# Turning softmax weights in row halves, and a new order of an attention visit, in a two-layer trunk on one core

## The chip, the cores and the metric

The kernel runs on one core of a Trainium2 chip. The metric is the device time of one execution in microseconds (us). An execution uses five engines that run side by side and wait for each other by semaphores: TensorE (PE, matmuls; its weight loads are shown as PEld), VectorE (DVE), ScalarE (ACT), GpSimd (POOL) and SyncE (SP), which here issues the weight DMAs. Matmul results land in PSUM, eight banks of 128 partitions by 512 fp32 words; everything else lives in SBUF. Each engine works through its own queue in order.

## The reference

The reference is a trunk of two layers over 256 latent tokens with 256 context tokens, width 1024, fp32. Each layer has a token-mixing part (a gated convolution branch beside an attention branch, both after a modulated norm and one combined projection) and a gated MLP. Cut to the attention, which is where the change lies:

```
s_win = einsum("bhqd,bhiqjd->bhqij", q_r, k_win) * scale + bias      # 16-wide window over the rows
s_ctx = einsum("bhqd,bhcd->bhqc", q_r, k_ctx) * scale                # all context keys
s = concatenate([s_win, s_ctx]);  p = softmax(s)
out = p_win @ v_win + p_ctx @ v_ctx                                  # latent queries
ctx_out = softmax(q_c k_c^T * scale) @ v_c                           # context queries, layer 0 only
```

There are 8 heads of 64 channels, taken as 4 pairs. In the last layer the context tokens only give keys and values, so nothing is computed for them as queries.

## The kernel before, in words

**Projections.** Weights come as units of 128x1024 fp32 by SP (tile `raw`, four buffers). ACT rounds a unit to fp32r (`whi`, L158) and DVE subtracts that from the unit (`wlo`, L159); a product of fp32 accuracy is then three matmuls (`mm3`, L177 to L179), each of a high or low weight part with a high or low part of the activations. A projection group is eight such triples into one PSUM bank. Between triples, `slot()` lets side work take a step: the taps of the convolution (DVE, L576) and the attention's visits.

**Attention.** The class `Attention` keeps three lists: `todo` (head pairs whose q and k are there), `soft` (pairs whose softmax weights `pp` are made, or on the way) and `pv` (turned weights `pT`, waiting for their product with V). A head pair gives one latent item of two query halves of 128; every two pairs give one context item in layer 0. A call of `step` that acts is one visit. It works off what the visit before left:

- `turn` (L476): the weights `pp` are [128 queries, 512 keys] per head and query half, and the product with V wants keys on partitions. Four 128x128 transposes on PE fill one bank, and one ACT copy (L485, for context items L490) takes the bank to `pT`. A visit has four such banks: tags sc, sc, pt, main in this order.
- `values` (L494): sixteen matmuls L502 of 256 moving columns into one bank, then per item an ACT cast `oh` (L508) and a DVE subtraction `ol` (L509).
- scores: `products` (L430) multiplies q by k in three high/low products for both heads of a pair; a head has 64 channels, so the two heads sit on partitions 0 to 63 and 64 to 127 and are multiplied in row halves of the PE array. The four banks are, in order, sc, sc, pt, main. Softmax follows: for latent items DVE adds the bias and finds the extremum (L448), ACT takes the exponential (L451) and scales (L454); for context items L462, L467 and L472.

Before, a visit is issued as turn, values, scores. A visit that has no weights to turn, or no values, or no scores leaves that stage out. In layer 0 the visits with a turn are six, the last of which has no scores; in layer 1 there are four, the last again without scores. Each layer ends with a visit of values alone.

**What sets the order.** The Tile framework takes instructions in the order of the program's calls, moves them by a priority of its own within what `tc.issue_after` allows, and fills in the semaphore waits. It also hands out the PSUM buffers of each tag (`BANKS`: main 4, sc 2, pt 1, po 1) in rotation; a new user of a bank waits for the last reader of the old one. Projection groups, the rotary step of q and k (DVE L747 to L750, ACT L753, DVE L754) and the attention's third and fourth banks all share main, so which bank a group gets depends on how many were taken before it.

**Who reads the banks.** ACT's copies L485 free the banks of a turn. In the same queue ACT has the whi casts, the sigmoids of the gates (L591 with the multiplication on DVE, L799), the copies of gate projections (L613), q and k's rounding (L753) and the softmax. DVE has the taps, the wlo subtractions and the rotary step.

**After layer 0's attention.** SP loads rows for the next modulation (`sb` from `in_crow`, L243); ACT computes on them (L245), DVE multiplies (L261), and PE's next step (L224) waits for the result of ACT L217.

Of the kernel before, what the change touches and what calls it, by code (L numbers as in the profile page):

```python
# [8 lines left out]
F32 = mybir.dt.float32  # L9
# [6 lines left out]
P = 128  # L16
# [3 lines left out]
S = 256  # L20
# [12 lines left out]
LAT, CTX = slice(0, S), slice(S, 2 * S)  # L33
# [12 lines left out]
def trunk(ctx: ExitStack, tc: tile.TileContext, xt, cvec, crow, wall, wada, params, bias_t, rope_t, out):  # L46
    nc = tc.nc
    pe, act, dve, pool, sp = nc.tensor, nc.scalar, nc.vector, nc.gpsimd, nc.sync
# [11 lines left out]
    def nm(s):  # L60
        uid[0] += 1
        return f"{s}_{uid[0]}"
# [3 lines left out]
    def psum(tag="main"):  # L66
        return psp.tile([P, 512], F32, tag=tag, bufs=BANKS[tag], name=nm(tag))

    def tmp(w=512):
        return tp.tile([P, w], F32, tag="t", bufs=5, name=nm("t"))  # L70
# [4 lines left out]
    def sl(w, i):  # L75
        return w[:, i * P : (i + 1) * P]
# [29 lines left out]
    start = ExitStack()  # L106
# [5 lines left out]
    ident = cp.tile([P, P], F32, name="ident")  # L112
# [260 lines left out]
    HALF = [slice(0, HD), slice(HD, P)]  # L373

    class Attention:
# [30 lines left out]
        def step(self, now=False):  # L406
            self.n += 1
            since = self.n - self.at
            if not now and (since < (4 if self.todo else 3 if self.soft else 2) or not self.todo and self.pairs < 4):
                return  # L410
            if self.todo and not now and self.n - self.todo[0][0] < 2:
                return
            self.at = self.n
            pv, self.pv = self.pv, []
            soft, self.soft = self.soft, []
            for what, its, pps in soft:
                with tc.issue_after(self.last.ins), tc.issue_after(self.done.ins):
                    self.turn(what, its, pps)
            for work in pv:
                self.values(*work, "sc" if work[0] == CTX and not (soft or self.todo) else "po")  # L420
            if self.todo:
                _, what, its = self.todo.pop(0)
                outs = [self.products(it, [psum(t) for t in tags]) for it, tags in zip(its, (("sc", "sc"), ("pt", "main")))]
                self.soft.append((what, its, [(self.scores if what == LAT else self.ctx_scores)(it, o) for it, o in zip(its, outs)]))

        def product(self, out, q, k, c, d):
# [48 lines left out]

        def turn(self, what, its, pps):  # L476

            pts = [self.eb.tile([P, 4, S], F32, tag="pT", bufs=4, name=nm("pT")) for _ in range(2)]
            for n, tags in enumerate((("sc", "sc"), ("pt", "main"))):
                for i, pp in enumerate(pps[n]):  # L480
                    pt = psum(tags[i])
                    if what == LAT:
                        for kt in range(4):
                            pe.transpose(sl(pt, kt), sl(pp, kt), ident)
                        act.copy(pts[i][:, :, n * P : (n + 1) * P], pt.rearrange("p (k q) -> p k q", k=4))  # L485
                    else:
                        for t in range(2):
                            for kt in range(2):
                                pe.transpose(pt[:, kt * S + t * P : kt * S + (t + 1) * P], sl(pp, 2 * t + kt), ident)
                        act.copy(pts[i][:, 2 * n : 2 * n + 2, :], pt.rearrange("p (k q) -> p k q", k=2))  # L490
            js = [its[0][0]] if what == LAT else [it[0] for it in its]
            self.pv.append((what, js, pts))

        def values(self, what, js, pts, bank):  # L494
            po = psum(bank)
            kts = range(4) if what == LAT else range(2, 4)
            for n, j in enumerate(js):
                c = slice(n * S, (n + 1) * S)
                for kt in kts:
                    for i in range(2):  # L500
                        h = 2 * j + i
                        pe.matmul(  # L502
                            po[i * HD : (i + 1) * HD, c], self.V[kt][:, h * HD : (h + 1) * HD],
                            pts[i][:, 2 * n + kt - kts[0], :], start=kt == kts[0], stop=kt == kts[-1],
                        )
            for n, j in enumerate(js):
                c = slice(n * S, (n + 1) * S)
                act.copy(self.oh[j][:, what], po[:, c])  # L508
                dve.tensor_tensor(self.ol[j][:, what], po[:, c], self.oh[j][:, what].bitcast(F32), ALU.subtract)  # L509
# [11 lines left out]
    for k in range(KD):  # L521
        sp.dma_start(x[k], xt[k])
        q = tmp()
# [19 lines left out]
    for l in range(DEPTH):  # L543
# [5 lines left out]
        with ExitStack() if last else start as e1a:  # L549
# [68 lines left out]
            with ExitStack() as e1b:  # L618
# [14 lines left out]
                if l == 0:  # L633

                    pv = [psum() for _ in range(4)]
# [81 lines left out]
                else:  # L717
                    sp.dma_start(rope, rope_t)
                    pg0 = [psum("sc") for _ in range(2)]
                    for uu in range(2):  # L720
                        wg = wunit(l, U_GLU0 + uu)
                        for i in range(2):
                            for kk in range(4):
                                k = 4 * uu + kk
# [44 lines left out]
                else:  # L769
                    wvs = [wunit(l, U_V + uu) for uu in range(4)]  # L770
                    for half in range(2):
                        pv = {t: psum() for t in (2 * half, 2 * half + 1)}
# [11 lines left out]
                n = 0  # L784
# [16 lines left out]
            with ExitStack() as e1c:  # L801
# [71 lines left out]
                for n, pc in branch(U_CO, sh_, sl_):  # L873
                    t = tmp()[:, :T]
# [60 lines left out]
        with ExitStack() as e2:  # L935
# [115 lines left out]
            for streams, ns in [((0, 1), range(NB)), *(((s,), range(NB, KD)) for s in range(NS))]:  # L1051
                wu = None
                c = slice(streams[0] * S, (streams[-1] + 1) * S)
                for n in ns:
                    ps = psum()
                    for k in range(KF):
                        t = n * KF + k
# [19 lines left out]
            if last:  # L1077
                std, rs = small([P, 2], "red"), small([P, 2], "rs")
                pt = psum("pt")
# [133 lines left out]
```

## Time and profile before

| what | value |
|---|---|
| median of 3 runs | 1129.97 us (1129.38 to 1132.16) |
| profiled execution, first to last instruction | 1127.4 us |
| granted TensorE clock, mean | 0.998 |
| PE busy | 1115.5 us (99%) |
| DVE busy | 906.5 us (80%) |
| ACT busy | 565.7 us (50%) |
| turns in the run | 10, of 16 transposes each (160) |
| visits with scores | 10 |

The profiled execution's own time is its span of 1127.4 us and what lies outside the first and last instruction, which the page does not show; the median of the runs is 2.6 us above that span.

The attention's visits, as the starts of their first matmuls on PE in us (the end is the start of the next projection group):

| layer, visit | turn | values | scores | next group |
|---|---|---|---|---|
| 0, first | | | 84.24 | 85.83 |
| 0, second | 102.69 | | 104.53 | 106.32 |
| 0, third | 112.00 | 113.84 | 115.72 | 117.57 |
| 0, last turn | 192.50 | 194.34 | | 196.22 |
| 0, last values | | 199.20 | | 201.08 |
| 1, second | 812.83 | | 814.66 | 816.45 |
| 1, third | 827.82 | 829.66 | 831.53 | 833.12 |
| 1, last turn | 858.47 | 860.31 | | 862.19 |

How to read the profile's lines: a timeline row gives the start and the covered time in us, the engine, the line of the kernel, the operation, output tile <- input tiles, the shape and the count; what stands in square brackets is the idle time of that engine before the row, and what ended it. A row of one source line gives the count, the shortest, median and longest duration in ns, and the first and last start in us. A PE matmul's duration includes its fill and drain, so the distance from one start to the next is what it costs in a sequence. "128*64" behind MATMUL means 128 rows and 64 columns of the PE array in use. The chain that ended last is followed back from the last instruction through what released each step.

### The profile page before, as it was taken

Reading aid. Unit: us, or ns where it says so; the run is one execution under the profiler, and the core shown is the slowest. Engines: PE = TensorE matmul, PEld = TensorE weight load, DVE = VectorE, ACT = ScalarE, POOL = GpSimd, SP = SyncE. Lnnn points to the kernel's source line nnn. Section 1 sums busy time; section 2 is a strip of 40 time slices with the busy share of each in tenths; the row PEclk is TensorE's granted clock in tenths of the full one; section 3 lists DMA queues with packets and bytes.
Section 4 is the critical chain, followed back from the end, with each engine's and each line's share of the span. In section 5 each row is a group of like instructions: output and inputs, shape, how many; then the busy total and the mean of one; then the engine's idle time right before and its main releaser. Section 6 shows DMA issues by size and latency. Waiting matters only on the chain.

```text
span 1127.4 us, 17780 instructions
## 1 busy us (share of the span) xinstructions
PE 1115.5 (99%) x6854; PEld 965.1 (86%) x6854; DVE 906.5 (80%) x1625; ACT 565.7 (50%) x937; POOL 17.2 (2%) x24
## 2 busy tenths in 40 slices
PE   9999999999999999999999999999999999999997
PEld 7678777787789988888888888989898999999997
DVE  4689999786778788888898555789996898988773
ACT  4347657542334543444334223544677667766642
POOL 0000000000000000000000000010000000000000
PEclk9999999999999999999999999999999999999999
DMA  8832231635734354545556656555533575665781
GB/s 325 310 100 89 92 117 38 200 99 198 248 120 145 110 170 133 184 152 155 165 181 205 214 188 197 176 194 174 154 109 120 180 247 175 187 193 182 213 274 57
DMA packets 53941, 190.83 MB, mean 169 GB/s; under 512 B 6240, under 2 KB 6496, under 8 KB 53856
## 3 DMA queue, kind: packets, MB, share of 16 engines
q1 hardware_dynamic: 53568, 189.65, 52.6%
q8 instruction: 54, 0.88, 0.3%
q14 instruction: 31, 0.25, 0.1%
q10 hardware_dynamic: 288, 0.04, 0.0%
HBM read 188.62 MB, written 1.05 MB: 168 GB/s over the span
## 4 chain that ended last, share of the span: by engine, by line
PE 85%; DVE 10%; DMA 2%; ACT 2%; issue 1%; POOL 0%; SPq 0%; DVEq 0%; ACTq 0%; POOLq 0%
PE main L177 25%; PE main L179 24%; PE main L178 24%; DVE cb L576 4%; PE main L629 4%; DVE wlo L159 2%; DMA raw<-in_wall 1%; PE sc L127 1%; PE sc L177 1%; PE sc L179 1%; PE sc L178 1%; PE po L200 1%; PE po L502 1%; DMA sb<-in_crow 1%; PE sc L430 0%
## 5 line engine op out<-in xcount | busy, mean ns | idle before, releaser
L177 PE MATMUL main<-h,whi 128*128 128x256 f32 (+1 forms) x1328 | 446.8, 337 | 0.0
L179 PE MATMUL main<-h,wlo 128*128 128x256 f32 (+1 forms) x1328 | 443.4, 335 | 0.5 <-DVE wlo L159 0.5
L178 PE MATMUL main<-h,whi 128*128 128x256 f32 (+1 forms) x1328 | 442.4, 333 | 0.0
L158 ACT CAST whi<-raw 128x1024 fp32r<-128x1024 f32 (+1 forms) x244 | 252.5, 1039 | 284.7 <-PE main L178 128.6
L159 DVE TENSOR_TENSOR wlo<-raw,whi 128x1024 fp32r<-128x1024 f32 (+1 forms) x244 | 293.7, 1209 | 113.3 <-ACT whi L158 108.6
L177 PEld LDWEIGHTS main<-h,whi 128*128 128x128 f32 x1328 | 249.5, 188 | 32.0 <-issue 3.9
L179 PEld LDWEIGHTS main<-h,wlo 128*128 128x128 f32 x1328 | 249.5, 188 | 28.9 <-DVE wlo L159 0.7
L178 PEld LDWEIGHTS main<-h,whi 128*128 128x128 f32 x1328 | 249.9, 188 | 28.1 <-issue 0.2
L576 DVE SCALAR_TENSOR_TENSOR cb<-u,par,cb 128x512 f32<-128x512 f32 (+1 forms) x240 | 140.6, 620 | 1.2
L261 DVE CUSTOM_DVE_ANT_0 t<-raw,sb,par 128x1024 bf16<-128x1024 f32 x100 | 126.9, 1280 | 1.4 <-ACT sb L245 1.2
L177 PE MATMUL main<-fh,whi 128*128 128x256 f32 (+1 forms) x386 | 123.0, 319 | 0.0
L178 PE MATMUL main<-fl,whi 128*128 128x256 f32 (+1 forms) x386 | 122.9, 319 | 0.0
L179 PE MATMUL main<-fh,wlo 128*128 128x256 f32 (+1 forms) x386 | 122.9, 318 | 0.0
L178 PEld LDWEIGHTS main<-fl,whi 128*128 128x128 f32 x386 | 72.7, 188 | 5.6
L177 PEld LDWEIGHTS main<-fh,whi 128*128 128x128 f32 x386 | 72.7, 188 | 5.6
L179 PEld LDWEIGHTS main<-fh,wlo 128*128 128x128 f32 x386 | 72.7, 188 | 5.5
L948 ACT ACTIVATE t<-main,par 128x512 f32<-128x512 f32 (+1 forms) x82 | 50.7, 669 | 35.3 <-PE main L179 35.3
L949 DVE SCALAR_TENSOR_TENSOR t<-main,par,t 128x510 f32<-128x510 f32 (+1 forms) x82 | 47.6, 616 | 8.2 <-ACT t L948 7.6
L952 DVE SCALAR_TENSOR_TENSOR t<-main,par,t 128x510 f32<-128x510 f32 (+1 forms) x82 | 46.6, 611 | 0.0
L356 ACT ACTIVATE h<-t,mod 128x256 fp32r<-128x256 f32 x56 | 25.2, 502 | 37.5 <-DVE t L355 37.4
L883 DVE SCALAR_TENSOR_TENSOR x<-main,mod,x 128x256 f32<-128x256 f32 x48 | 22.1, 480 | 23.6 <-PE main L179 23.4
L629 PE MATMUL main<-whi,h 128*128 128x512 f32 x128 | 40.6, 402 | 0.0
(217 smaller groups left out, 1198.0 us busy)
## 6 DMA issues: line engine op xcount, KB each, us to landing
raw<-in_wall SPq DMA_DIRECT2D x239, 512.0 KB, 4.2
raw<-in_wada SPq DMA_DIRECT2D x88, 512.0 KB, 4.4
bias<-in_bias_t SPq DMA_DIRECT2D x8, 640.0 KB, 4.4
row<-in_wada SPq DMA_DIRECT2D x8, 512.0 KB, 4.8
sb<-in_crow SPq DMA_DIRECT2D x5, 512.0 KB, 6.1
x<-in_xt SPq DMA_DIRECT2D x8, 256.0 KB, 4.6
raw<-in_wall SPq DMA_DIRECT2D x8, 256.0 KB, 6.8
out<-t SPq DMA_DIRECT2D x3, 256.0 KB, 2.1
```

Of the source, the lines that this page charges most:

```text
L158: act.copy(hi[:, c], r[:, c])
L159: dve.tensor_tensor(lo[:, c], r[:, c], hi[:, c].bitcast(F32), ALU.subtract)
L177: pe.matmul(ps, w[0], xh, start=start, stop=False)
L178: pe.matmul(ps, w[0], xl, start=False, stop=False)
L179: pe.matmul(ps, w[1], xh, start=False, stop=stop)
L261: dve.tensor_tensor_reduce(tmp().bitcast(BF16), r, v, 1.0, pr(l, BADA + n, 1), ALU.mult, ALU.add, mods[l][:, n, s : s + 1])
L356: high = act.activation(hi[:, c], y[:, c], AF.Identity, bias=b)
L576: dve.scalar_tensor_tensor(cb[j], src, w, cb[j], ALU.mult, ALU.add)
L629: pe.matmul(pv[t], h1[n == 1][k][:, c], w[n == 2][:, b], start=k + n == 0, stop=k == KD - 1 and n == 2)
L948: act.activation(c, pv_, AF.Identity, bias=pr(l, FDB + t, 1), scale=w[1])
L949: dve.scalar_tensor_tensor(c[:, :, 1:], pv_[:, :, : S - 1], w[0], c[:, :, 1:], ALU.mult, ALU.add)
L952: dve.scalar_tensor_tensor(c[:, :, : S - 1], pv_[:, :, 1:], w[2], c[:, :, : S - 1], ALU.mult, ALU.add)
```

## The change

Three things change, all within `Attention`.

1. `step` issues values, then turn, then scores (before: turn, values, scores). The values of a visit use what the visit before turned, as before.
2. The four banks of the scores are main, main, sc, sc (before: sc, sc, pt, main).
3. `turn` splits each 128x128 transpose into two on 64 rows: rows 0 to 63 of `pp` against the upper left 64x64 of the identity, rows 64 to 127 against the lower right. The two go into two banks, one per row half; a bank now holds both heads' four slices of one row half. So a turn has 32 transposes of 64 moving columns in 16 pairs (320 instead of 160 in the run), still four banks with the same tags, still four ACT copies of 128x512. Both banks of a pair are complete only after the eighth pair. The copies write runs of 64 columns. `pT` is one tile [128, 2, 4, 256] with two buffers instead of two tiles [128, 4, 256] with four.

Arithmetic is the same, and no DMA is added or removed. Because of new lines, what stood from L500 on is one line further down in the changed kernel (L502 becomes L503, L509 becomes L510); the transposes are L485 for both kinds of item, and the copies L488 and L491.

```diff
             pv, self.pv = self.pv, []
             soft, self.soft = self.soft, []
+            for work in pv:
+                self.values(*work, "sc" if work[0] == CTX and not (soft or self.todo) else "po")
             for what, its, pps in soft:
                 with tc.issue_after(self.last.ins), tc.issue_after(self.done.ins):
                     self.turn(what, its, pps)
-            for work in pv:
-                self.values(*work, "sc" if work[0] == CTX and not (soft or self.todo) else "po")
             if self.todo:
                 _, what, its = self.todo.pop(0)
-                outs = [self.products(it, [psum(t) for t in tags]) for it, tags in zip(its, (("sc", "sc"), ("pt", "main")))]
+                outs = [self.products(it, [psum(t) for t in tags]) for it, tags in zip(its, (("main", "main"), ("sc", "sc")))]
...
         def turn(self, what, its, pps):
 
-            pts = [self.eb.tile([P, 4, S], F32, tag="pT", bufs=4, name=nm("pT")) for _ in range(2)]
+            pT = self.eb.tile([P, 2, 4, S], F32, tag="pT", bufs=2, name=nm("pT"))
             for n, tags in enumerate((("sc", "sc"), ("pt", "main"))):
+                outs = [psum(t).rearrange("p (i s q) -> p i s q", i=2, s=4) for t in tags]
                 for i, pp in enumerate(pps[n]):
-                    pt = psum(tags[i])
+                    for s in range(4):
+                        src = s if what == LAT else s % 2 * 2 + s // 2
+                        for pt, r in zip(outs, HALF):
+                            pe.transpose(pt[:, i, s], sl(pp, src)[r], ident[r, r])
+                for pt, r in zip(outs, HALF):
                     if what == LAT:
-                        for kt in range(4):
-                            pe.transpose(sl(pt, kt), sl(pp, kt), ident)
-                        act.copy(pts[i][:, :, n * P : (n + 1) * P], pt.rearrange("p (k q) -> p k q", k=4))
+                        act.copy(pT[:, :, :, n * P + r.start : n * P + r.stop], pt)
                     else:
-                        for t in range(2):
-                            for kt in range(2):
-                                pe.transpose(pt[:, kt * S + t * P : kt * S + (t + 1) * P], sl(pp, 2 * t + kt), ident)
-                        act.copy(pts[i][:, 2 * n : 2 * n + 2, :], pt.rearrange("p (k q) -> p k q", k=2))
+                        to = pT[:, :, 2 * n : 2 * n + 2].rearrange("p i k (t q) -> p i (k t) q", t=2)
+                        act.copy(to[:, :, :, r], pt)
...
-        def values(self, what, js, pts, bank):
+        def values(self, what, js, pT, bank):
...
-                            pts[i][:, 2 * n + kt - kts[0], :], start=kt == kts[0], stop=kt == kts[-1],
+                            pT[:, i, 2 * n + kt - kts[0]], start=kt == kts[0], stop=kt == kts[-1],
```

More of the change, by code (lines that the diff above doesn't have):

```diff
@@ L476, in turn @@
         def turn(self, what, its, pps):
-            pts = [self.eb.tile([P, 4, S], F32, tag="pT", bufs=4, name=nm("pT")) for _ in range(2)]
+            pT = self.eb.tile([P, 2, 4, S], F32, tag="pT", bufs=2, name=nm("pT"))
             for n, tags in enumerate((("sc", "sc"), ("pt", "main"))):
+                outs = [psum(t).rearrange("p (i s q) -> p i s q", i=2, s=4) for t in tags]
                 for i, pp in enumerate(pps[n]):
-                    pt = psum(tags[i])
+                    for s in range(4):
[3 more added lines that the diff above has]
+                for pt, r in zip(outs, HALF):
                     if what == LAT:
-                        for kt in range(4):
-                            pe.transpose(sl(pt, kt), sl(pp, kt), ident)
-                        act.copy(pts[i][:, :, n * P : (n + 1) * P], pt.rearrange("p (k q) -> p k q", k=4))
-                    else:
-                        for t in range(2):
-                            for kt in range(2):
-                                pe.transpose(pt[:, kt * S + t * P : kt * S + (t + 1) * P], sl(pp, 2 * t + kt), ident)
-                        act.copy(pts[i][:, 2 * n : 2 * n + 2, :], pt.rearrange("p (k q) -> p k q", k=2))
+                        act.copy(pT[:, :, :, n * P + r.start : n * P + r.stop], pt)
+                    else:
+                        to = pT[:, :, 2 * n : 2 * n + 2].rearrange("p i k (t q) -> p i (k t) q", t=2)
+                        act.copy(to[:, :, :, r], pt)
             js = [its[0][0]] if what == LAT else [it[0] for it in its]
-            self.pv.append((what, js, pts))
-        def values(self, what, js, pts, bank):
+            self.pv.append((what, js, pT))
+        def values(self, what, js, pT, bank):
             po = psum(bank)
```

## The prediction

> **What bounds the kernel now.** I read the page's busy shares first, then the chain that ended last, then the timelines of the attention visits on TensorE (PE), ScalarE (ACT) and VectorE (DVE).
>
> ```profile
> span 1127.4 us, 17780 instructions
> PE 1115.5 (99%) x6854; PEld 965.1 (86%) x6854; DVE 906.5 (80%) x1625; ACT 565.7 (50%) x937; POOL 17.2 (2%) x24
> PE 85%; DVE 10%; DMA 2%; ACT 2%; issue 1%; POOL 0%; SPq 0%; DVEq 0%; ACTq 0%; POOLq 0%
> ```
>
> PE is busy 99% of the span and carries 85% of the chain; DVE carries 10%, in stretches where PE waits or is paced by it. So what the change does to PE's order is paid or gained nearly one for one, except where another engine then ends last. The attention visits stand between projection groups of PE (L177 to L179). This is a first turning visit without values, and the next one, with values:
>
> ```profile
> 102.69 1.04 PE L484 MATMUL sc<-ident,pp 128*128 128x128 f32 x8
> 103.56 0.60 PE L484 MATMUL pt<-ident,pp 128*128 128x128 f32 x4
> 104.53 1.17 PE L430 MATMUL sc<-qk,qk 64*128 64x512 f32 x6
> 106.32 0.50 PE L177 MATMUL main<-h,whi 128*128 128x512 f32 x1
> 112.00 1.03 PE L484 MATMUL sc<-ident,pp 128*128 128x128 f32 x8
> 113.84 1.95 PE L502 MATMUL po<-pT,V 128*64 128x256 f32 x16
> 115.72 1.21 PE L430 MATMUL sc<-qk,qk 64*128 64x256 f32 x12
> 117.57 0.50 PE L177 MATMUL main<-h,whi 128*128 128x512 f32 x1
> ```
>
> The first column is the start, the second the time covered. A turn (16 transposes) lasts 104.53 − 102.69 = 1.84 us: eight take 103.56 − 102.69 = 0.87, so 0.109 each, and some 0.1 at the end where PE goes over to 64-row tiles. Values last 115.72 − 113.84 = 1.88 and scores 1.79 (106.32 − 104.53) for latent queries, 1.85 for context queries. There are ten turns in the run (two layers), eight of them followed by scores in the same visit.
>
> **The change, part by part.** (a) Half transposes. Each 128x128 transpose becomes two on 64 rows, at row positions 0 and 64, writing two banks. What a pair of them costs (X) no row of before shows. The nearest rows (the first three from the scores at 115.72, then two of a projection):
>
> ```profile
> 116.89 0.28 PE L430 MATMUL pt<-qk,qk 64*128 64x256 f32 x1
> 117.00 0.28 PE L430 MATMUL main<-qk,qk 64*128 64x256 f32 x1
> 117.01 0.28 PE L430 MATMUL pt<-qk,qk 64*128 64x256 f32 x1
> ...
> 816.67 0.28 PE L178 MATMUL main<-h,whi 128*128 128x256 f32 x1
> 816.79 0.28 PE L179 MATMUL main<-h,wlo 128*128 128x256 f32 x1
> ```
>
> ```profile
> 15.80 0.20 PEld L224 LDWEIGHTS pt<-ident,t 128*128 128x128 f32 x2
> L484 PEld LDWEIGHTS sc<-ident,pp x64: 138/141/144, 102.5 to 859.1; 128*128 128x128 f32 x64
> L502 PEld LDWEIGHTS po<-pT,V x144: 132/137/137, 113.8 to 869.4; 128*64 128x64 f32 x144
> L517 PEld LDWEIGHTS pt<-one,t x40: 186/192/192, 7.3 to 14.5; 128*128 128x128 f32 x40
> ```
>
> Side by side: L430's halves start 0.01 apart and the same half follows after 0.12, as long as one full-height matmul of 256 columns (816.67 to 816.79). Row halves therefore do run at the same time, their loads of 128 columns too. Load: two L224 loads of 0.141 (like L484's) cover 0.20 together, so the second began 0.06 behind the first; an ordinary load of the same size, L517, is 0.05 longer, and one of 64 columns, L502, is as short as the transpose's. So a transpose's load holds the array about 0.055. Moving: 64 columns instead of 128 at 0.109 make 0.055. Lower end: X = 0.056, both halves concurrent. Middle: X = 0.109, where the two loads go one behind the other. Upper end: X = 0.218, where each half costs a whole transpose and none overlap. I take 0.056, the row of L430 being nearest (same tile position, same halves). A turn is then 16 × 0.056 + 0.1 for entering the mode + 0.1 for the drain = 1.10 alone, 1.01 where scores follow in the same mode: about 0.85 less than now, at most 8.5 over ten turns.
>
> The Trainium skill, "TensorE: Matmul & The Clock Gate", section "LDWEIGHTS (loading the stationary operand)", says that a load's time goes by the columns (P / 1.2 ns), and that a load of few rows costs as much as a full one; for 128 columns that is an estimate of 0.107 us, a pair would gain nothing if its loads were serial, and the sum would end at the second rival's time. The trace disagrees for transposes (0.06 between L224's two loads), and agrees for L517.
>
> (b) Copies. ACT still makes four copies of 128x512 a turn, but the first two become ready together after 8 pairs, and the last two after 16:
>
> ```profile
> 102.65 1.05 ACT L158 CAST whi<-raw 128x1024 fp32r<-128x1024 f32 x1 [2.31 <-PE main L178]
> 103.61 1.06 ACT L485 COPY pT<-sc 128x512 f32<-128x512 f32 x2
> 105.04 0.61 ACT L485 COPY pT<-main 128x512 f32<-128x512 f32 x1
> 114.33 0.60 ACT L591 ACTIVATE t<-main 128x512 f32<-128x512 f32 x1
> 114.82 1.07 ACT L485 COPY pT<-sc 128x512 f32<-128x512 f32 x2
> ```
>
> The fourth copy begins 1.43 behind the first (105.04 − 103.61), so one follows another by 0.475 and four need 2.0, and behind a whi cast of 0.95 they cannot begin before 103.61. The writes go in runs of 64 columns; I price the copy as now (0.58 to 0.61), bounded by −0.05 and +0.1 each: whatever it is, it is hidden only if the copies are.
>
> (c) Order and banks. Values now stand ahead of the turn (nothing of them is added: 1.88 as before; pT's four tiles become two double ones, same bytes; no DMA moves). That takes away the 1.88 us of values that lay between the copies and the scores. Scores take main, main and then sc, sc, and the last pair must wait for the first two copies of this turn, the next projection group now and then for the fourth. Three kinds of visit follow.
>
> First kind, copies free to run. At 102.69: pairs until 103.79, scores into main until 104.5, sc from the second copy's end (103.61 + 1.06 = 104.67), six matmul pairs at 0.116 more: the group starts near 105.70, when the fourth copy (105.65) frees its bank: −0.62. At 112.00: values to 113.88, pairs to 114.98, ACT busy with its table load and the sigmoid L591 (114.33) and a cast of values (0.33, from L508 below) until 115.15, second copy ends 116.2, scores end 117.07 against 117.57: −0.50. Three more visits are taken at their mean, −0.56 (two in layer 0, one in layer 1); in one of layer 0 such a cast, which waits for DVE, falls between the copies: −0.14, the mean less 0.42. Were X 0.109, they would be −0.2, −0.2, about 0 and +0.1.
>
> Second kind, waits on DVE in layer 1:
>
> ```profile
> 816.10 0.42 DVE L750 TENSOR_TENSOR t<-t,t 128x256 f32<-128x256 f32 x1
> 820.98 0.42 DVE L754 SCALAR_TENSOR_TENSOR qk<-main,qk 128x256 fp32r<-128x256 f32 x1
> 816.45 0.38 PE L177 MATMUL main<-h,whi 128*128 128x256 f32 x1
> 832.03 0.42 ACT L753 ACTIVATE qk<-t 128x256 fp32r<-128x256 f32 x1 [1.25 <-DVE t L750]
> 833.12 0.39 PE L177 MATMUL main<-h,whi 128*128 128x256 f32 x1
> ```
>
> At 816.45 the next group found a free bank. With scores in main it takes the bank of a K projection, which DVE gives back by L754 behind L750: 816.43 + 0.42 = 816.85, +0.40. In the next visit ACT's qk<-t (832.03, behind DVE) stands ahead of the four copies in the changed order: copies from 832.36, the second done 833.42, scores end 834.2 against 833.12, +1.08, of which the first 0.40 is already in: +0.68. Both hold for X = 0.056 and 0.109, since PE is not what ends last.
>
> Third kind, the visits that end a layer's attention:
>
> ```profile
> 194.83 0.63 ACT L799 ACTIVATE g<-g 128x512 f32<-128x512 f32 x1
> 195.36 1.05 ACT L490 COPY pT<-sc 128x512 f32<-128x512 f32 x2
> 198.32 0.39 ACT L508 CAST oh<-po 128x256 fp32r<-128x256 f32 x1
> 199.10 2.02 ACT L158 CAST whi<-raw 128x1024 fp32r<-128x1024 f32 x2
> 199.20 1.95 PE L502 MATMUL sc<-pT,V 128*64 128x256 f32 x16
> ```
>
> Now ACT copies after one sigmoid (L799). In the changed kernel's order all four sigmoids (0.53 from start to start), a cast of values (0.33) and a whi cast (0.95) stand ahead: 194.83 + 2.12 + 0.33 + 0.95 = 198.2 for the first copy, 199.3 for the end of the second, and the last values, which could start at 198.5, wait for it: 199.3 and more against 199.20, +0.15. The like in layer 1, where more sigmoids stand there, is taken at the same +0.15.
>
> (d) A stop behind layer 0's visits:
>
> ```profile
> 191.89 7.84 DVE L576 SCALAR_TENSOR_TENSOR cb<-u,par,cb 128x512 f32<-128x512 f32 x10
> 200.64 1.22 DVE L159 TENSOR_TENSOR wlo<-raw,whi 128x1024 fp32r<-128x1024 f32 x1
> 202.27 6.08 DMA sb<-in_crow
> 211.72 0.26 ACT t L217
> ```
>
> The first two rows are DVE's timeline, the others are pieces of the chain of that stretch. SyncE issues this transfer behind DVE's L159 at 200.6; PE waits for what follows at 212.0. So an earlier PE gains only as far as that transfer comes earlier. In the changed order two taps fewer (0.78 each) stand ahead of that L159: at most 1.57.
>
> The sum for X = 0.056: layer 0 −0.62 − 0.50 − 2 × 0.56 − 0.14 + 0.15 = −2.2, cut to −1.57 by the transfer; layer 1 +0.40 + 0.68 − 0.56 + 0.15 = +0.67. Together −0.9 us: 1127.4 becomes 1126.5. The median of the runs before, 1129.97, is 2.6 above the profiled span; with the same 2.6 it is 1129.1. What I call the same is within 0.3%, 3.4 us: about what a measurement of this kernel can tell.
>
> The Trainium skill, "TensorEngine Tiling (Array Packing)", section "PSUM Bottleneck", speaks against the change: tiling speeds TensorE up, not the emptying of PSUM, so the copy may become the bound. ACT's four copies of 2.0 us beside a turn of 1.1 agree with it; the third rival below is this mechanism carried through.
>
> **The rivals.** *Faster by more:* the first kind's gain in all ten visits, neither DVE's nor ACT's queue getting in the way. Then 10 × 0.6 = 6, so 1124.0, if the stretch before the transfer (d) gives way too. For it: PE is 99% busy and my waits rest on the old clock times of ACT and DVE, which an earlier PE also moves. Against it: ACT's order ahead of the copies is fixed.
>
> *The halves don't overlap* (X = 0.109): the change doesn't do what it says. Layer 0 −0.2 − 0.2 + 0 + 0 + 0.1 + 0.15, layer 1 +0.40 + 0.68 + 0.1 + 0.15: +1.2, so 1131.2, still the same within 0.3%.
>
> *Slower, the copies bind:* in each of the eight visits with scores the last sc scores or the next group wait for the second or fourth copy, behind what else ACT has, as I found only at 833.12. Price +0.7 each where it happens, 8 × 0.7 + 0.3 = +5.9, so 1135.9. It decides once ACT begins the copies more than about 1.2 us after the pairs are ready, since the scores into main cover 0.7 and the turn gives 0.85. For it: the cover of 1.88 is gone, and ACT's table loads and casts stand ahead in most visits. Against: ACT is 50% busy, and at 102.69 the copies start at once.
>
> *Slower, each half costs a whole transpose* (X = 0.218): 10 × 16 × 0.109 = +17.4, less nothing: 1147.4. L430's pairs speak against it.
>
> **How the numbers follow.** Forecast case 0.32 (1129.1, its own range 1126.5 to 1132), no overlap 0.12, faster by more 0.26, copies bind 0.23, whole price 0.07. Same: 0.32 + 0.12 less a little at its edges, 0.41. Faster: 0.27. Slower: 0.23 + 0.07 + 0.02 = 0.32. The range, 1123.0 to 1138.0, reaches to the faster rival and past the copies' price, and leaves out the whole price, two in a hundred below, and as many of dearer copies.
>
> **What would show it.** (a) Turn of 16 pairs: starts 0.056 apart and a stage of 1.0 to 1.1 us if right; 0.109 and 1.84 if the halves don't overlap. (b) Copies in pairs of 0.475 spacing, the sc scores starting right at the second one's end. (c) At the visit that is now at 812.83 a stop of PE of about 0.4 ended by DVE's qk, and one of about 1 in the next ended by ACT's pT. (d) The stop before L224 at 212 still there, a little longer. Wrong would be: copies that start late in most visits (the slower rival), a copy much longer than 0.61 because of its 64-column runs, or other banks that set free late between the visits, which I did not price.

## The result and the profile after

The changed kernel takes 1134.05 us in the median of 17 runs, the kernel before 1130.17 us in 17 runs of the same session: a ratio of 1.003, 95% interval 1.002 to 1.004. It is slower by some 0.3%, where the prediction said 1129.1 and no measurable change. A later session on the same two kernels gave 1.0021 (1.0006 to 1.0037).

The mean granted TensorE clock of a run goes with most of the spread from run to run. In the 35 runs of the kernel before in the later session, the seven with a clock of 0.998 took 1129.0 us on average, the eight with 0.993 took 1134.7. The product of a run's span and clock takes that out: 1124.6 on average over these 35 runs (standard deviation 0.7), 1126.8 for the changed kernel in both sessions (17 and 12 runs). So some 2.2 us of the loss are not the clock; the rest, some 1.7 in the first session and nothing in the second, differs between sessions. Below, "product" means this number.

The page of the changed kernel, parts 1, 3 and 4:

```profile
span 1131.4 us, 18110 instructions
PE 1112.0 (98%) x7014; PEld 958.8 (85%) x7014; DVE 906.8 (80%) x1625; ACT 566.0 (50%) x937; POOL 18.7 (2%) x24
q8 instruction: 55, 0.90, 0.3%
PE 77%; DVE 15%; ACT 4%; issue 2%; DMA 2%; POOL 0%; DVEq 0%; ACTq 0%; SPq 0%; POOLq 0%
```

PE is busy 3.5 us less than before and the span is 4.0 longer: the work on PE did shrink, but PE stands idle for 7.5 us more, and more of the chain goes over DVE (15%, 10% before) and ACT (4%, 2% before). There are 160 more matmuls and 160 more loads. The row of queue q8 (packets, MB, share) will matter later; before it had 54 packets, 0.88 MB together.

The turn itself, in the timeline of PE and in the rows of its line:

```profile
102.13 0.71 PE L485 MATMUL sc<-ident,pp 64*128 64x64 f32 x16
103.15 0.94 PE L430 MATMUL main<-qk,qk 64*128 64x512 f32 x6
105.05 0.51 PE L177 MATMUL main<-h,whi 128*128 128x512 f32 x1
```

```profile
L485 PEld LDWEIGHTS sc<-ident,pp x160: 134/138/142, 102.1 to 861.2; 64*128 64x128 f32 x160
L488 ACT COPY pT<-sc x16: 568/590/616, 103.0 to 866.9; 128x512 f32<-128x512 f32 x16
```

A turn takes 103.15 − 102.13 = 1.02 us instead of 1.84, and its two halves run together at some 0.06 a pair. The copies take 0.59, as before. This visit ended 0.62 us earlier, against the projection ahead of it, than before.

**Where the time went.** Every PE matmul outside the visits exists in both kernels, so its start can be compared. The table gives what each stretch adds to the span against the first profile of before, in us, by the starts of the same two matmuls at its two ends. "Start" is everything up to 80 us, "layer 0" the attention from there to 235, "737" the stretch from 720 to 760, "layer 1" from 760 to 890, "933" from 890 to 945. Everything else is within 0.16. The second half of the table belongs to the experiments below.

| kernel | start | layer 0 | 737 | layer 1 | 933 |
|---|---|---|---|---|---|
| changed | −0.65 | −0.36 | +0.74 | +0.72 | +3.54 |
| changed, second profile | +0.46 | −0.37 | +0.69 | +0.72 | +0.99 |
| before, second profile | −0.20 | −0.03 | +0.01 | +0.01 | +1.24 |
| pairs alone | +0.64 | +0.64 | +0.74 | +0.61 | +3.84 |
| pairs and banks | +3.34 | +0.87 | +0.89 | +0.62 | +0.52 |
| pairs and order | −0.51 | −0.36 | +0.67 | +1.41 | +2.58 |
| order and banks | +3.26 | −1.19 | −0.26 | +0.68 | +0.80 |
| order alone | +3.28 | −0.45 | +0.06 | +0.92 | +0.72 |
| banks alone | −0.07 | −0.33 | −0.04 | +0.33 | +0.29 |
| order and banks, layer 0 only | +3.20 | −1.19 | +0.09 | +0.03 | +0.75 |
| changed, 31 more fillers | +7.77 | −0.32 | −0.12 | +0.72 | +1.12 |
| before, fillers in four | +4.55 | −0.46 | −0.32 | −0.01 | +3.99 |
| before, 48 more fillers | +14.60 | −0.15 | +0.60 | 0.00 | +0.99 |

The start differs from profile to profile of one and the same kernel (−0.65 and +0.46), in part with the clock of the first 25 us; it says nothing of the change. The attention, which the prediction was about, comes out at +0.36 in both profiles of the changed kernel. What it had no step for is +0.7 at 737 and +1.0 to +3.5 at 933, two places with no attention in them.

The waits in the visits, PE's rows (in brackets the idle time before them and what ended it):

```profile
114.87 0.97 PE L430 MATMUL main<-qk,qk 64*128 64x256 f32 x11 [0.79 <-ACT t L592]
166.58 0.96 PE L430 MATMUL sc<-qk,qk 64*128 64x512 f32 x5 [1.31 <-ACT pT L488]
199.43 2.07 PE L503 MATMUL sc<-pT,V 128*64 128x256 f32 x16 [1.32 <-ACT pT L491]
816.67 0.39 PE L177 MATMUL main<-h,whi 128*128 128x256 f32 x1 [1.09 <-DVE qk L755]
832.63 1.45 PE L430 MATMUL sc<-qk,qk 64*128 64x512 f32 x6 [0.66 <-ACT pT L488]
```

The second of these, seen from ACT:

```profile
163.83 0.59 ACT L488 COPY pT<-sc 128x512 f32<-128x512 f32 x1 [0.25 <-PE sc L485]
165.66 0.37 ACT L509 CAST oh<-po 128x256 fp32r<-128x256 f32 x1 [1.25 <-DVE ol L510]
165.93 0.59 ACT L488 COPY pT<-sc 128x512 f32<-128x512 f32 x1
```

Between the first copy and the second stands a cast of values that waits for DVE's L510, which stands behind a tap and a wlo of DVE. So the second copy comes 2.1 us behind the first instead of 0.48, and the sc scores with it.

The stop before L326 (the matmul that sums the squares `ss` for a norm) at 737, PE's rows in before and in the changed kernel:

```profile
737.19 0.58 PE L326 MATMUL pt<-one,ss 128*128 128x1 f32 x4 [0.23 <-DVE ss L312]
```

```profile
736.95 0.58 PE L326 MATMUL pt<-one,ss 128*128 128x1 f32 x4 [0.98 <-DVE ss L312]
```

And the weight transfer from which the chain reaches it, over ACT's L158 and DVE's L159 and L312, again before and changed:

```profile
730.64 3.66 DMA raw<-in_wall
```

```profile
729.65 4.42 DMA raw<-in_wall
```

The orders of SP, ACT and DVE around it are the same in both; the transfer takes 0.76 longer.

### The profile page after: what moved, and what is told of

It reads as the page before. It is cut to its first block, busy times and chain, and to the rows that moved or that the text cites. A ratio compares the mean times of both kernels' runs of the same rounds, so it can differ in the third digit from the quotient of the medians.

```text
span 1131.4 us, 18110 instructions
## 1 busy us (share of the span) xinstructions
PE 1112.0 (98%) x7014; PEld 958.8 (85%) x7014; DVE 906.8 (80%) x1625; ACT 566.0 (50%) x937; POOL 18.7 (2%) x24
## 4 chain that ended last, share of the span: by engine, by line
PE 77%; DVE 15%; ACT 4%; issue 2%; DMA 2%; POOL 0%; DVEq 0%; ACTq 0%; SPq 0%; POOLq 0%
PE main L177 22%; PE main L179 22%; PE main L178 22%; DVE cb L577 6%; PE main L630 4%; DVE wlo L159 3%; DMA raw<-in_wall 2%; PE sc L177 1%; PE sc L179 1%; PE sc L178 1%; PE sc L127 1%; ACT whi L158 1%; DVE main L448 1%; PE po L200 1%; DVE qk L755 1%
## 5 line engine op out<-in xcount | busy, mean ns | idle before, releaser
L158 ACT CAST whi<-raw 128x1024 fp32r<-128x1024 f32 (+1 forms) x244 | 252.6, 1039 | 283.4 <-DMA raw<-in_wall 126.9
L159 DVE TENSOR_TENSOR wlo<-raw,whi 128x1024 fp32r<-128x1024 f32 (+1 forms) x244 | 293.3, 1208 | 118.1 <-ACT whi L158 116.4
```

The source lines that it names most:

```text
L158: act.copy(hi[:, c], r[:, c])
L159: dve.tensor_tensor(lo[:, c], r[:, c], hi[:, c].bitcast(F32), ALU.subtract)
```

## The experiments

**The three parts apart.** The theory was that the waits of order and banks eat what the pairs gain; the rival, that a shorter attention gains nothing because stops behind it swallow it. First the pairs alone, as an edit of the changed kernel (of the long line only the changed piece is shown, here and below):

```diff
-            for work in pv:
-                self.values(*work, "sc" if work[0] == CTX and not (soft or self.todo) else "po")
             for what, its, pps in soft:
                 with tc.issue_after(self.last.ins), tc.issue_after(self.done.ins):
                     self.turn(what, its, pps)
+            for work in pv:
+                self.values(*work, "sc" if work[0] == CTX and not (soft or self.todo) else "po")
...
-zip(its, (("main", "main"), ("sc", "sc")))
+zip(its, (("sc", "sc"), ("pt", "main")))
```

> Only the turn by pairs; the order (turn, values, scores) and the banks of the scores as before. Theory (the waits that order and banks make eat the gain): each turn is 1.0 us instead of 1.84, and in the eight visits where values follow the turn the copies have 1.9 us of cover, so each such visit is 0.8 shorter; the two without values 0.4. That is some 7 us over the ten visits; of layer 0's part (4.5) only about 1.5 gets past the wait for the in_crow transfer, layer 1's 3 stays: 4 to 5 us faster than before. Rival (a shorter attention gains nothing, the stops behind it that end with a weight transfer swallow it, and the loss of the changed kernel comes from there): the visits are shorter by the same amounts, the time is within 1 us of before.

Measured: 1.0042 (1.0025 to 1.0059), the slowest of the three; product 1127.2. Both were wrong. PE's rows show that pairs alone make waits too:

```profile
104.88 1.44 PE L430 MATMUL sc<-qk,qk 64*128 64x512 f32 x6 [0.25 <-ACT pT L488]
116.64 1.46 PE L430 MATMUL sc<-qk,qk 64*128 64x256 f32 x12 [0.83 <-ACT pT L488]
193.85 0.27 PE L485 MATMUL pt<-ident,pp 64*128 64x64 f32 x1 [1.16 <-ACT pp L472]
```

With values between, the copies still end later than PE (116.64), and in the last turn PE is so early that ACT has not scaled the weights (193.85). The attention as a whole is 1.25 longer than before, not 7 shorter.

Pairs with the banks, old order (only the first part of the diff above):

> Pairs and the new banks for the scores (main, main, sc, sc), but the old order turn, values, scores. Theory: the waits that the banks make stay (PE behind the sigmoid of the gated unit in the third visit of layer 0, behind q and k's rounding in two visits of layer 1: 0.5 to 1 us each, 2 in all), those of the order go (1.3 at the fifth visit and 1.3 before the last values of layer 0): 2 to 3 us faster than before. Rival (stops behind swallow it): within 1 us of before.

Measured: 1.0032 (1.0018 to 1.0046), product 1127.0: slower, where 2 to 3 us faster or no difference had been expected. Pairs with the order, old banks (only the second part):

> Pairs and the new order values, turn, scores, but the old banks for the scores (sc, sc, pt, main). Theory: the first score matmuls now need the first two copies, and the last two banks the third and fourth, with only the turn itself as cover, so each visit with scores waits some 1 to 1.5 us for ACT: the visits lose 0.3 to 0.6 each against before, 2 to 5 us slower than before, more than the changed kernel. Rival (the banks alone make the loss): faster than before by 1 to 3 us.

Measured: 1.0026 (1.0008 to 1.0044), product 1127.3. Layer 1 lost 1.41, the most of all, by waits for the copies, as the theory had it; layer 0 did not (−0.36). The longest of these waits:

```profile
832.89 1.45 PE L430 MATMUL sc<-qk,qk 64*128 64x512 f32 x6 [1.39 <-ACT pT L488]
```

Besides these, the changed kernel once more:

> The changed kernel once more, for a second profile beside the three others. If the late transfer before the norm of layer 1 (a stop of PE of 2.5 us that ends at 936.4) and the lower clock behind it belong to this kernel, both are there again and the time is 3 to 4 us above before; if they were a chance of the profiled execution, the profile is without them, 2 to 3 us shorter, and the time still tells some 1 to 4 us.

Measured: 1133.81, ratio 1.0021 (1.0006 to 1.0037). The attention and the stop at 737 are the same as in the first profile to 0.05; at 933 there was a shorter stop and no low clock.

**The parts without pairs, and before again.** If pairs are what the four have in common, the same order and banks with whole transposes should be harmless. This is the kernel before with both edits; "order alone" has only the first of them, "banks alone" only the second, and "before" is the kernel before, unchanged:

```diff
+            for work in pv:
+                self.values(*work, "sc" if work[0] == CTX and not (soft or self.todo) else "po")
             for what, its, pps in soft:
                 with tc.issue_after(self.last.ins), tc.issue_after(self.done.ins):
                     self.turn(what, its, pps)
-            for work in pv:
-                self.values(*work, "sc" if work[0] == CTX and not (soft or self.todo) else "po")
...
-zip(its, (("sc", "sc"), ("pt", "main")))
+zip(its, (("main", "main"), ("sc", "sc")))
```

> Order values, turn, scores and the new banks, with the whole transposes of before. Theory (pairs shorten the turn by 0.83, the waits of order and banks are there without them): each turn 1.84, waits behind the copies and main banks as in the changed kernel or shorter by up to 0.8, so about +1 to +3 us against before. Rival (the pairs are what makes it slower): within 1 us of before.

> The order values, turn, scores alone, whole transposes and old banks of scores. The copies have only the second half of the turn as cover (0.9 us) before the first score matmul needs their bank. Theory: 0.3 to 1 us lost in each of the visits with scores, +3 to +6 us. Rival (the pairs make it slower): within 1 us of before.

> The banks main, main, sc, sc for the scores alone. Theory: PE waits behind the sigmoid (third visit of layer 0) and behind q and k's rounding (layer 1), 0.3 to 1 us each at two or three places, +1 to +2 us. Rival (the pairs make it slower): within 1 us of before.

> The kernel before once more, for a second profile of it. Theory (the five profiles with pairs stop PE longer at two places that the change doesn't touch, 0.7 to 1.1 us before the norm at 737 and 0.5 to 2.2 before the one at 933, because of the change): this profile is like the first one of before at both places, within 0.2 and 0.4 us, with the same time as before. Rival (the first profile of before was a lucky one): this one shows the longer stops as well, and the change costs only what its visits show.

Measured: order and banks 0.9988 (0.9973 to 1.0003), order alone 1.0008 (0.9991 to 1.0026), banks alone 0.9992 (0.9977 to 1.0007), before 0.9995 (0.9981 to 1.0009). None differs from before. In the product: 1124.7, 1125.4, 1124.9 and 1124.7 against 1124.6. So order and banks cost at most 0.8 by themselves, and every kernel with pairs stands 2.2 to 2.7 above before. The second profile of before settles half of the question: at 737 it is like the first, so +0.7 there goes with the pairs (five profiles of five with pairs, none of five without); at 933 it is 1.24 above the first one, so the first was short there by chance, and the six profiles without pairs and with the start as before (one of them from the last experiment) average +0.6.

**Why a stop 500 us behind the visits.** Two rows of the page (PE and q8) give a clue: 2 x 6854 PE instructions on 54 packets before are one packet per 254, of 0.88 MB / 54 = 16 KB. Queue q8 of kind "instruction" thus looks like PE's program being fetched as it is used up. The view of the DMA queues, cut to the stretch of the chain's transfer, shows no such packet in before (730.64 to 734.30), and one in the changed kernel (729.65 to 734.07):

```profile
q1 hardware_dynamic: 158, 0.58, 63.6%
```

```profile
q1 hardware_dynamic: 187, 0.70, 63.5%
q8 instruction: 1, 0.02, 1.6%
```

In before the packet starts at 727.71, ahead of the transfer; 1.4% of 16 engines for the 4 us from 726 to 730 is 0.9 us of one engine:

```profile
q8 instruction: 1, 0.02, 1.4%
```

The other profiles agree. SP issues this transfer and its neighbours at the same distances in all fourteen. In the five with pairs a packet starts 1.2 to 1.4 us behind the transfer's start, which then takes 4.36 to 4.60; in the six without pairs and with the start as before it starts 2.9 to 4.2 us ahead, and the transfer takes 3.43 to 3.76.

By 737 six turns have run, with 6 x 32 = 192 more PE instructions, and the packets stand three quarters of their distance earlier. That is a theory one can test without touching the attention: add PE instructions at the start and see whether the stop goes or comes. The start has 31 filler matmuls, whose results nothing reads; a filler is two matmuls and two loads in the trace (L127: 62 and 62). With the changed kernel:

```diff
-        for _ in range(n):
-            mm = pe.matmul(sl(warm, 0), ident, ident, start=True, stop=True)
+        for _ in range(2 * n):
+            mm = pe.matmul(warm[:64, :64], ident[:, :64], ident[:, :64], start=True, stop=True)
```

> The changed kernel, with each of the 31 filler matmuls of the start (128x128 of the identity, results never read) split into two of 64x64 moving and stationary columns: 62 PE instructions more at about the same PE time. In all profiles a packet of 16 KB on the instruction queue comes every 256 or so PE instructions. Theory (with pairs such a packet falls into the weight transfer that PE waits for at 737 and makes it 0.7 us longer, since 192 more PE instructions have run by then; 62 more make it 256, a whole packet): the packet moves some 3.5 us ahead of that transfer, the transfer takes 3.7 us again instead of 4.4, the stretch from 720 to 760 loses 0.0 against before instead of 0.7. Rival (the pairs slow it otherwise): 0.7 as before this edit.

It added 124 instructions, not 62 (two of each for a filler), which puts the packet 60 and not 254 instructions ahead of where before has it, at 731.8 where the transfer begins at 738.1; either way it is out of the transfer. The chain's transfer and PE's row:

```profile
738.09 3.58 DMA raw<-in_wall
```

```profile
744.57 0.58 PE L326 MATMUL pt<-one,ss 128*128 128x1 f32 x4
```

3.58 us, no idle time before L326 in the timeline, and −0.12 in the stretch instead of +0.7: with all its pairs, the stop is gone. The kernel as a whole is slower, 1.0063 (1.0045 to 1.0082), with a clock that stayed low for 13.7 us at the start (+7.77 there). Its product, 1127.0, is no lower than the changed kernel's, but 0.9 of it, counted in the same way, comes from the start; so the times of the runs with other fillers don't weigh the 0.7, and only the stretch does. The other direction, the kernel before with fillers split into four of 32 columns:

> The kernel before, with each filler matmul split into four of 32 columns: 186 PE instructions more at the start, no pairs. Theory (the packet's place makes the stop): by 737 the packets stand as in the kernels with pairs (192 more), one falls into the weight transfer there, and the stretch from 720 to 760 loses 0.7 against before without any pair; the attention's visits are as before. Rival (the pairs themselves, or where the scheduler puts things, make it): 0.0 there, within 0.1.

This missed its aim: 372 instructions instead of 186, so the packet stood ahead of the transfer (at 726.8, the transfer from 734.7, 3.35 us) and nothing was lost at 737. It showed something else. A packet now falls right on the start of the transfer that the norm at 933 waits for, and that stop is the longest of all, in a kernel without pairs:

```profile
940.09 0.71 PE L326 MATMUL pt<-one,ss 128*128 128x1 f32 x4 [2.89 <-DVE ss L312]
```

Ratio 1.0059 (1.0039 to 1.0078); of the 8.0 us of the profile, 4.6 come from the start. The same test with the right count, 48 fillers more, which is 192 instructions:

```diff
+    fills = [0]
+
     def busy(n):
         for _ in range(n):
-            mm = pe.matmul(sl(warm, 0), ident, ident, start=True, stop=True)
+            fills[0] += 1
+            for w in (64, 64) if fills[0] <= 14 else (64, 32, 32):
+                mm = pe.matmul(warm[:w, :w], ident[:, :w], ident[:, :w], start=True, stop=True)
```

> The kernel before with its 31 fillers split into two or three narrower ones, 48 more; a filler is four PE instructions in the traces (two loads, two matmuls), so 192 more instructions, as many as the six turns by pairs of layer 0 add (the run before split into four, which made 372, so that its packet stood elsewhere). No pairs, order and banks as before. Theory (the packet's place): a 16 KB packet falls into the weight transfer before the norm at 737, the transfer takes 4.4 us or more instead of 3.7, and the stretch from 720 to 760 loses 0.6 to 0.8 against before. Rival (pairs or the scheduler's other choices make the stop): 3.7 us and 0.0, within 0.1. The start is some 5 us longer for both, as with the other splits.

The chain's transfer, and the queue's row for its stretch (745.10 to 749.40):

```profile
745.10 4.30 DMA raw<-in_wall
```

```profile
q8 instruction: 1, 0.02, 1.4%
```

The packet is in, the transfer takes 4.30, and the stretch loses 0.60, with no pair in the kernel. (Its time, 1.014 (1.010 to 1.018), is the start's: half clock for 24 us.) So the stop at 737 is set by where the packets of this queue fall, PE's program as it seems, and the pairs only move them. Each direction rests on one profile.

**At 933** the same holds less cleanly. A packet lies in the transfer that ends the chain there in the changed kernel (both profiles), in pairs alone, pairs and banks, pairs and order, and overlaps its start in the fillers in four: these add 3.54, 0.99, 3.84, 0.52, 2.58 and 3.99. The seven other profiles besides the first of before, none with a packet in it, add 0.29 to 1.24. The transfer itself takes 4.51 to 5.96 with the packet and 4.22 to 5.24 without, so the two groups overlap, and no run moved the packet there alone: the packet as cause is not shown here. Part of the difference is the clock: after four of the six stops it was halved for 3.4 us. The stretch 936 to 941 in the first and in the second profile of the changed kernel (the third number from the end is the granted TensorE clock):

```profile
936.00:941.00 5.00, 4.60 (x26) 4.60 (x27) 3.18 (x6) 2.43 (x4) 0.70 (x1) 0.66 0.85 267
```

```profile
936.00:941.00 5.00, 4.51 (x38) 4.51 (x39) 3.96 (x7) 2.93 (x5) 0.70 (x1) 1.00 0.91 288
```

That costs 1.46 us of the 3.54. It came after stops of 1.73 to 3.17 between two matmuls' starts, and not after 1.92 at the same place in the second profile of before, or 2.03 before L224 with pairs and banks, so the length alone does not decide it; what else does stays open.

**A version of its own.** The one gain the runs showed is layer 0's −1.19 with order and banks and whole transposes; layer 1 loses by them. So in layer 0 only:

```diff
+            def val():
+                for work in pv:
+                    self.values(*work, "sc" if work[0] == CTX and not (soft or self.todo) else "po")
+
+            if self.l == 0:
+                val()
             for what, its, pps in soft:
                 with tc.issue_after(self.last.ins), tc.issue_after(self.done.ins):
                     self.turn(what, its, pps)
-            for work in pv:
-                self.values(*work, "sc" if work[0] == CTX and not (soft or self.todo) else "po")
+            if self.l:
+                val()
...
+zip(its, (("sc", "sc"), ("pt", "main")) if self.l else (("main", "main"), ("sc", "sc")))
```

> Whole transposes; the new order and the new banks in layer 0 alone, layer 1 as before. From the run of order and banks in both layers, whose layer 0 gained 1.2 us by the end of the wait for in_crow and whose layer 1 lost 0.7: layer 0 gains 1.2 again, layer 1 loses nothing, 1.2 us faster than before in span times clock (0.1%). If the gain of layer 0 was a chance of one profile, no difference.

Measured: 0.9994 (0.9984 to 1.0004), no difference by the times. By the product, 1123.5 (0.6, 12 runs) against 1124.5 (0.6, 17 runs), 1.1 us less; layer 0 −1.19 again, layer 1 +0.03.

## Why the prediction was wrong

Wrong: 1129.1, most likely the same, against 1134.05 and slower by 0.3%. That the range held the time is owed to its width, up to 1138 for dearer copies; none of the rivals was the cause. Step by step:

- **The pair (X).** Right: 0.056 was taken and a turn is 1.02 (1.01 was worked out). The rivals with 0.109 and 0.218 are out. On the load rule of the Trainium skill, "TensorE: Matmul & The Clock Gate", section "LDWEIGHTS (loading the stationary operand)", read as the time for which a load holds the array, the trace disagrees here: a pair, two loads of 128 columns and two moves of 64, follows the one before it by some 0.06 us, below the estimate of 0.107 for one load.
- **Copies.** Right in price (0.59) and in that they bind.
- **First kind of visit.** Three as forecast: −0.62 at 102 (−0.62), −0.48 and −0.59 at 134 and 179 (−0.56 each). Two with the wrong sign: the visit at 112 gave +0.72 for −0.50, since the main bank of its scores belonged to a gated unit whose sigmoid (L592) stands behind a whi cast and a table load; the step saw that ACT was busy until 115, but charged only the copies for it and not the bank. The visit at 162 gave +1.06 for −0.14: the cast between the copies was named, and priced by its 0.42 instead of by DVE's wait ahead of it.
- **Second kind, layer 1.** Right in sum: +0.46 and +0.67 (forecast +0.40 and +0.68), then −0.56, and +0.15 for the end of layer 1. Together +0.72 for +0.67. The stops themselves, 1.09 and 0.66, are not the 0.4 and 1 that had been named as signs.
- **Third kind, layer 0.** The moment was right (last values at 199.43, forecast 199.3). The sum was not: that wait ends by ACT's queue, and so swallows what PE had gained up to there instead of adding 0.15 to it. Last turn and last values together gave +0.90.
- **(d)** Half right: the transfer came earlier and PE's stop before L224, which was forecast to stay, vanished, a gain of 1.3 that made up for the lost visits (PE's rows, before and changed, below). The runs with whole transposes show that it comes from order and banks (−1.19), with no pairs needed. Layer 0: −0.36 for −1.57.

```profile
212.03 0.44 PE L224 MATMUL pt<-ident,t 128*128 128x128 f32 x2 [1.13 <-ACT t L217]
```

```profile
211.09 0.38 PE L224 MATMUL pt<-ident,t 128*128 128x128 f32 x2
```

- **The steps that failed** are two. In part (c), the waits of the first kind of visit: the sum took −0.50 and −0.14 for the visits at 112 and 162, and they gave +0.72 and +1.06, by waits for the gate's sigmoid and for DVE. With what the wait at the end of layer 0 swallowed and what (d) gave back, attention came out at +0.36 where −0.9 was forecast, 1.3 us of error. In part (a), the 160 added transposes were costed by their time on PE, and everything behind the attention was put at nothing without a reason. The runs showed +0.7 at 737, from the place of a 16 KB packet, and a longer stop at 933, in some executions with low clock behind it. There the cause stays open: a packet lies in the transfer in all five profiles with pairs, but the times with and without one overlap, and it was not isolated. With time at half clock counted half, as in the product, the stretch at 933 adds 1.4 on average in the two profiles of the changed kernel and 0.6 in the six without pairs, 0.8 more. Then 0.36 + 0.7 + 0.8 is 1.9 for a measured 2.2, an estimate from few profiles.

The slower rival ("the copies bind") described what happened in single visits, but its price of 5.9 did not arise, and with order and banks but no pairs there was no loss to speak of. The caution of the Trainium skill's "TensorEngine Tiling (Array Packing)", section "PSUM Bottleneck", that copies become the bound, is borne out by the waits for pT (1.31 and 0.66 above, 0.83 with pairs alone).

## What to carry to other kernels

Where PE waits a handful of times per execution for a transfer or another engine, shortening PE's work in between moves little; ask of each stop whether its end moves. A wait that ends at a time set by another queue wipes out the gains before it: do not add it to them. And instructions are a cost of their own: doubling the count of small ones moves the packets of the instruction queue, and a stop far from the edit can grow or go; compare two profiles of each kernel, stretch by stretch, before giving a cause.

## What was not expected of the hardware

There is a packet of 16 KB on the instruction queue for about every 254 PE instructions, beside the transfers of the weights: in fourteen profiles the 512 KB transfer at 737 took 4.30 to 4.60 us with such a packet in it and 3.35 to 3.76 without. The granted clock was halved for 3.4 us behind some stops of PE of 1.7 to 3.2 us in the middle of a busy execution. At the start it was halved for 10.2 to 23.9 us in the three profiles with narrow fillers, and for 0 to 6.8 us in the others.
